# Retention and attention scores in 128-row products throughout, and the Fourier products ahead of the key projection

## The chip, the core and the metric

The kernel runs on one core of a Trainium2 chip. The metric is the device time of one execution in microseconds (us). Of the kernel before there are three timed runs, 2704.53 to 2708.25 us with a median of 2707.93 us, and one profiled execution of 2709.11 us, in which the span from the first to the last instruction is 2707.0 us.

## What is computed

The reference is a backbone of two layers over 512 latent tokens and 256 context tokens of width 1024, all in float32. Each layer is a half-step SwiGLU, a token mixing of four groups of heads side by side, and a second half-step SwiGLU. The change lies in the token mixing, which in short is:

```python
pl = split(n_lat @ w_in); pc = split(n_ctx @ w_in)      # ten groups of columns
# retention, 4 heads of 64: rotary q, k; decay both ways around each token
scores = einsum('bhcld,bhcmd->bhclm', qc, kc) * intra
o      = einsum('bhclm,bhcme->bhcle', scores, vc) + carried state
fft_lat = real(fft2(pl[4]))                             # over tokens and over 64 features
# attention: 4 query heads, 2 key heads, RMS norm and rotary on q and k
s = einsum('bkgqd,bknd->bkgqn', q, k) * HEAD_DIM ** -0.5
o = einsum('bkgqn,bknd->bkgqd', softmax(s), v)          # keys: context and latent tokens
gm_lat  = gelu(u) * (w_s @ layer_norm(gelu(v)) + b_s)
mix_lat = concatenate([ret_lat, fft_lat, att_lat, gm_lat]) @ w_out
```

The context stream goes through the same mixing in layer 0; in layer 1 only the latent stream does.

## The kernel before

Nearly all matrix products work on pairs of a rounded high part and a low part (the rest), both in a 32-bit format (`fp32r`) that TensorE takes at full rate; a product of two such pairs is three products (high by high, high by low, low by high). In the trace the products of the projections, the SwiGLUs and the scores are on the lines L241 and L243 (of the helper `mm`), transposes on L282, and all that VectorE (DVE), ScalarE (ACT) and GpSimd (POOL) do on L127.

The scores use a packing of their own. A head has 64 features, so half of the 128 rows of a product would be empty. `stack` (line 1485) takes the transposed heads, two in one PSUM bank of 128 partitions, and fills tiles for them. For keys the 64 rows of a head's own half hold the high part and the other 64 rows the low part (`lo is None`: two copies on ACT, two subtractions on DVE). For queries all 128 rows of `keys` hold the high part twice (four copies), and the low part goes into the 64 rows of the head's own half of `lo` (two subtractions). A score tile is then two products into one bank: one over 128 rows (high and low parts of the keys by the high part of the queries) and one over 64 rows, the slice `b0:b0 + 64` (high part of the keys by the low part of the queries). In retention the keys are the stationary operand and 512 latent (or 256 context) queries stream; in attention 128 queries are stationary and up to 512 keys stream, so that a tile of 768 keys is a product of 512 and one of 256 columns, each with its 64-row partner.

Per layer, `mixing` (line 1952) issues the projections in this order: retention's queries, keys and values for two pairs of heads (`qk0`, `rv`, `qk1`), the gate, the gMLP inputs, the Fourier input `f`, attention's queries `aq`, keys and values `akv`; then the Fourier products over tokens (`dft` weights), then the first half of the output projection (`wout`, sections 3 and 0) and the second (sections 1 and 2). After a projection an epilogue (rotary or norm on DVE and ACT, transposes on PE, `stack`) prepares its tiles. `ret_core`, `att_core`, `gm_core` and `four_tail` are separate tasks.

The order on each engine is decided when the program is built. A scheduler runs these tasks as generators; each waits until the times that a cost model gives for its operands are reached, and then emits its instructions. Tasks with a lower number go first, and the main sequence of projections, with the number 9, fills the time that the others leave to PE. The model counts the columns of a product and not its rows. Long-lived tiles come out of 20 slots of one size (`uget`, `uf`); a task that finds none free waits. Weights are read in the order of `wplan` (line 486), at most four blocks ahead.

Of the kernel before, what the change touches and what calls it, by code (L numbers as in the profile page):

```python
# [15 lines left out]
P = 128  # L16
# [19 lines left out]
def f32v(ap):  # L36
    return ap.bitcast(F32)
# [103 lines left out]
class Kernel:  # L141
# [344 lines left out]
    def wplan(self):  # L486
# [86 lines left out]
        for l in range(2):  # L573
            ffn(l, 1)
            win(l, "qk0", [(0, 128), (256, 128)])
            win(l, "rv", [(512, 256)])
            win(l, "qk1", [(128, 128), (384, 128)])
            win(l, "rg", [(768, 256)])
            win(l, "gu", [(1792, 256)])
            win(l, "gv", [(2048, 256)])  # L580
            win(l, "f", [(1024, 256)])
            win(l, "aq", [(1280, 256)])
            win(l, "akv", [(1536, 256)])
            dft(l)
            wout(l, (3, 0))
            wout(l, (1, 2))
            ffn(l, 2)
# [897 lines left out]
    def stack(self, keys, lo, src):  # L1485

        own = (slice(0, 64), slice(64, 128))
        yield self.at(src)  # L1490
        for h in range(2):
            self.A("copy", keys[own[h], h], src[own[h]])
        if lo is not None:
            for h in range(2):
                self.A("copy", keys[own[1 - h], h], src[own[h]])
        yield self.at(keys)
        for h in range(2):
            self.V("tensor_sub", keys[own[1 - h], h] if lo is None else lo[own[h]], src[own[h]], f32v(keys[own[h], h]))

    def turn_task(self, jobs, dsts, flag):  # L1500

# [9 lines left out]
    def ret_qk(self, p):  # L1511

        def epi(t, bank, ps):
            yield (lambda: ("mc", self.layer) in self.flags)
            y, a, b = yield from self.tw(3)
            yield self.at(bank)
            yield self.vidle(self.SE)
            yv = y.rearrange("p (t c) -> p t c", t=2)
            self.rope(lambda tt: yv[:, tt].rearrange("p (h s c) -> p h s c", h=4, s=2), ps.rearrange("p t (h s c) -> p t h s c", h=4, s=2),
                      self.rrope[:, t:t + 2, 0, :], self.rrope[:, t:t + 2, 1, :], 4, a, b)  # L1520
            self.dead(bank, a, b)
            self.spawn(task(t, y, yv), 1)

        def task(t, y, yv):
            tt = slice(t * P, (t + 2) * P)
            jobs, dsts = [[yv[:, i, 128:256] for i in range(2)]], [(self.rk[p][:, :, tt], None)]
            if t < 4:
                jobs.append([yv[:, i, 0:128] for i in range(2)])
                dsts.append((self.rq[p][:, 0:2, tt], self.rq[p][:, 2, tt]))
            elif self.layer == 0:  # L1530
                jobs.append([yv[:, i, 0:128] for i in range(2)])
                dsts.append((self.rqx[:, p, 0:2], self.rqx[:, p, 2]))
            yield from self.turn_task(jobs, dsts, ("rqk", p))
            self.dead(y)
        return epi
# [25 lines left out]
    def ret_core(self, l, p):  # L1561

        if p == 1:
            yield (lambda: ("rD", l) in self.flags)
        Dn = []
        for i in range(2):
            x = yield from self.uget([P, 1536])
            yield (lambda: min(self.xdone.values()) == KT)
            yield from self.decay(l, 2 * p + i, x)
            Dn.append(x)  # L1570
        if p == 0:
            self.ro = yield from self.uget([P, 2, TOK])
            self.flags.add(("rD", l))
        yield (lambda: self.count.get(("rqk", p), 0) == 6 and self.count.get("rv", 0) == 6)
        q, k = self.rq[p], self.rk[p]
        yield self.rdy(q, k, self.rv[p], Dn[0])
        parts = [(0, 512, [4, 5, 0, 1, 2, 3])]
        if l == 0:
            parts.append((512, 256, [4, 5]))

        def soft(ps, nq, D, w0, t, ok):
            sh, sl = t
            yield self.at(ps[:, :nq])
            self.V("scalar_tensor_tensor", ps[:, :nq], ps[:, :nq], 0.125, D[:, w0:w0 + nq], op0=ALU.mult, op1=ALU.mult)
            yield from self.split_t(sh[:, :nq], sl[:, :nq], ps[:, :nq])
            self.dead(ps)
            ok.append(True)

        for i in range(2):
            h = 2 * p + i  # L1590
            b0 = 64 * i
            D = Dn[i]
            yield self.rdy(D)
            for q0, nq, keys in parts:
                po = None
                pend = []
                for ki in range(len(keys) + 2):
                    if ki < len(keys):
                        kt = keys[ki]
                        t = yield from self.tw(2, [F32R, F32R])  # L1600
                        ps = yield from self.bank()
                        kk = slice(kt * P, (kt + 1) * P)
                        qx = q if q0 == 0 else self.rqx[:, p]
                        self.mm(ps[:, :nq], k[:, i, kk], qx[:, i], True, False)
                        self.mm(ps[:, :nq], k[b0:b0 + 64, i, kk], qx[b0:b0 + 64, 2], False, True)
                        w0 = 896 + 128 - (kt - 4) * P if kt >= 4 and q0 == 0 else 384 - (kt % 4) * P
                        ok = []
                        self.spawn(soft(ps, nq, D, w0, t, ok), 1)
                        pend.append((ki, kt, t, ok))
                        yield  # L1610
                    if len(pend) > self.RP or ki >= len(keys) and pend:
                        kj, kt, t, ok = pend.pop(0)
                        if po is None:
                            po = yield from self.bank()
                        yield (lambda: ok)
                        yield self.rdy(t[1][:, :nq])
                        self.mmv(po[:, :nq], self.rv[p][:, kt, i], t[0][:, :nq], t[1][:, :nq], kj == 0, kj == len(keys) - 1)
                        self.dead(t[0], t[1])
                        yield
                self.spawn(self.ret_fold(l, p, self.ro[b0:b0 + 64, p, q0:q0 + nq], po[:, :nq]), 1)  # L1620
            self.uf(Dn[i])
        self.uf(self.rq[p], self.rk[p], self.rv[p])
        if p == 1 and l == 0:
            self.uf(self.rqx)

    def ret_fold(self, l, p, dst, po):
        yield from self.fold(dst, po)
# [52 lines left out]
    def att_qk(self, l, which):  # L1680
# [13 lines left out]
        def task(t, x, sq):  # L1694
# [34 lines left out]
            if which == 0:  # L1729

                jobs = [[y[:, i, j * P:(j + 1) * P] for i in range(2)] for j in range(2)]
                dsts = [(self.aq[j][:, :, tt], self.aq[2][:, j, tt]) for j in range(2)]
            else:
                jobs = [[y[:, i, 0:128] for i in range(2)]]
                dsts = [(self.ak[:, :, tt], None)]
# [5 lines left out]
    def att_core(self, l):  # L1741
# [10 lines left out]
        def scores():  # L1752
            for it, (t0, nk, h) in enumerate(its):
                yield (lambda: it - done["t"] < 4)
                b0 = 64 * (h // 2)
                kv = h // 2
                k0 = 0 if nk == 768 else 512
                for tt in range(2):
# [5 lines left out]
                    for c0 in range(0, nk, 512):  # L1764
                        c1 = min(c0 + 512, nk)
                        ks = slice(k0 + c0, k0 + c1)
                        self.mm(ps[:, c0:c1], self.aq[h % 2][:, kv, qs], self.ak[:, kv, ks], True, False)
                        self.mm(ps[:, c0:c1], self.aq[2][b0:b0 + 64, h % 2, qs], self.ak[b0:b0 + 64, kv, ks], False, True)
                    self.spawn(soft(it, tt, pa[it % 4][:, tt, :nk], ps, nk), 1)
                    yield  # L1770

# [180 lines left out]
    def mixing(self, l, norm):  # L1952
# [20 lines left out]
            self.count["rv"] = self.count.get("rv", 0) + 2  # L1973

        for p in range(2):
            self.rq[p] = yield from self.uget([P, 3, 512], F32R)
            self.rk[p] = yield from self.uget([P, 2, TOK], F32R)
            if p == 0 and l == 0:
                self.rqx = yield from self.uget([P, 2, 3, 256], F32R)
            if p == 0:  # L1980
                self.spawn(self.ret_core(l, 0), 2)
                for i in range(2):
# [86 lines left out]
            self.count["f"] = self.count.get("f", 0) + 2  # L2069

        yield from self.proj(l, [("f", epi_f, t) for t in lat])
        self.aq = yield from self.ugets(3, [P, 2, TOK], F32R)
        qk = self.att_qk(l, 0)
        yield from self.proj(l, [("aq", qk, t) for t in lat])
        self.ak = yield from self.uget([P, 2, TOK], F32R)
        self.av = yield from self.uget([P, 6, 2, 2, 64], F32R)
        kv = self.att_qk(l, 1)
        yield from self.proj(l, [("akv", kv, t) for t in every])
        for k in range(4):
            self.uf(*self.xt[k])  # L2080
        self.spawn(self.att_core(l), 2)
        chunks = [LAT, CTXC] if l == 0 else [LAT]
# [18 lines left out]
        if l == 0:  # L2101
# [9 lines left out]
            self.A("copy", self.fT[:, :, 512:768], ps.rearrange("p (e c) -> p e c", e=2))  # L2111
            self.dead(ps)
        self.uf(fh, fl)
        self.spawn(self.four_tail(l), 2)
        yield (lambda: ("mix", l, 3) in self.flags and ("mix", l, 0) in self.flags)
        yield from self.wout(l, (3, 0), chunks, G)
# [135 lines left out]
```

## Time and profile before

| | |
|---|---|
| median of three timed runs | 2707.93 us |
| profiled execution | 2709.11 us |
| its span | 2707.0 us |
| PE busy (matmuls) | 2611.7 us, 96% |
| weight loads (PEld) | 2442.5 us, 90% |
| DVE / ACT / POOL busy | 74% / 47% / 50% |
| token mixing, layer 0 and layer 1 | about 608 to 954 us and 2050 to 2326 us |

A matmul's end is modelled in the profile, so that a busy PE may still be waiting between two products. Whether it does is read from the distance between the starts of neighbouring rows of the timeline, and from the idle time ahead of a weight load on PEld: every product has one load of its own.

### The profile page before, as it was taken

To read this page: it belongs to the slowest core of one execution; us is meant where nothing else is said; L and a number is where in the kernel's file an instruction comes from. 1 tells how busy PE (TensorE), PEld (TensorE's weight loads), DVE (VectorE), ACT (ScalarE), POOL (GpSimd) and SP (SyncE) were. 2 spreads that over 40 slices of the span, in tenths; PEclk is the share of its full clock that TensorE was granted. 3 is DMA by queue.
4 is the path that set the end of the run, shared out by engine and by line. 5 is a ranking of instruction groups with operands and counts; after the bars stand their busy time and mean duration, and the time that the engine had idled before them with its cause. 6 is when DMAs were issued, how large, how long until landed. Compare 5 with 4: busy or idle time off the path is not lost.

```text
span 2707.0 us, 45375 instructions
## 1 busy us (share of the span) xinstructions
PE 2611.7 (96%) x17308; PEld 2442.5 (90%) x17308; DVE 2014.0 (74%) x3473; ACT 1269.3 (47%) x2620; POOL 1345.2 (50%) x1094
## 2 busy tenths in 40 slices
PE   7999999999999999999999989999999999999998
PEld 5888999998797988888999989999999797999998
DVE  5765787877578785656887877878878677877776
ACT  5433444455645554343444534444446545544445
POOL 3535666733222253546765547668734231654443
PEclk9999999999999999999999999999999999999999
DMA  8456222121111145553123111221232111122332
GB/s 289 138 167 210 71 70 87 63 81 55 51 44 47 40 144 191 172 187 109 63 63 102 55 47 63 64 93 63 63 104 63 51 60 42 48 94 94 105 99 78
DMA packets 242778, 252.62 MB, mean 93 GB/s; under 512 B 12188, under 2 KB 226432, under 8 KB 242560
## 3 DMA queue, kind: packets, MB, share of 16 engines
q1 hardware_dynamic: 236304, 246.82, 28.5%
q10 hardware_dynamic: 6256, 2.90, 0.4%
q8 instruction: 136, 2.23, 0.3%
q14 instruction: 82, 0.67, 0.1%
HBM read 247.59 MB, written 2.10 MB: 92 GB/s over the span
## 4 chain that ended last, share of the span: by engine, by line
PE 72%; DVE 18%; issue 3%; ACT 2%; DMA 2%; POOL 2%; SPq 0%; ACTq 0%; DVEq 0%; POOLq 0%
PE b L241 41%; PE b L243 28%; DVE u L127 7%; DVE w L127 6%; DVE t L127 3%; PE b L254 2%; PE b L282 2%; DVE H L127 2%; DMA raw<-in_ffn_w_gu_dram 1%; ACT w L127 1%; DMA u<-in_ada_w_dram 1%; ACT u L127 1%; ACT t L127 1%; POOL u L127 0%; POOL raw L127 0%
## 5 line engine op out<-in xcount | busy, mean ns | idle before, releaser
L241 PE MATMUL b<-u,w 128*128 128x384 f32 (+1 forms) x8736 | 1465.3, 326 | 30.7 <-DVE u L127 21.4
L241 PEld LDWEIGHTS b<-u,w 128*128 128x128 f32 x8736 | 1424.0, 189 | 61.0 <-DVE u L127 28.9
L127 ACT CAST w<-raw 128x512 fp32r<-128x512 f32 x949 | 578.9, 621 | 626.9 <-PE b L241 255.2
L127 DVE TENSOR_TENSOR w<-raw,w 128x512 fp32r<-128x512 f32 x688 | 663.0, 972 | 231.4 <-ACT w L127 219.6
L127 POOL TENSOR_TENSOR raw<-raw 128x512 f32<-128x512 f32 x416 | 616.9, 1504 | 397.2 <-DMA raw<-in_ffn_w_gu_dram 138.1
L127 POOL TENSOR_TENSOR w<-raw,w 128x512 fp32r<-128x512 f32 x261 | 371.0, 1433 | 543.6 <-ACT w L127 495.2
L243 PE MATMUL b<-u,w 128*128 128x256 f32 (+2 forms) x3888 | 590.9, 309 | 17.7 <-ACT u L127 5.8
L243 PEld LDWEIGHTS b<-u,w 128*128 128x128 f32 x3888 | 543.0, 194 | 44.8 <-issue 10.2
L127 DVE SCALAR_TENSOR_TENSOR H<-b,modG,H 128x128 f32<-128x128 f32 (+3 forms) x832 | 368.5, 474 | 154.1 <-PE b L243 85.4
L243 PE MATMUL b<-w,u 128*128 128x256 f32 x2172 | 286.6, 288 | 1.8 <-DVE w L127 1.8
L243 PEld LDWEIGHTS b<-w,u 128*128 128x128 f32 x2172 | 270.0, 192 | 12.0 <-issue 6.8
L127 ACT COPY t<-b 128x384 f32<-128x384 f32 (+5 forms) x287 | 123.5, 431 | 209.6 <-PE b L241 98.1
L127 ACT CAST u<-u 128x384 fp32r<-128x384 f32 (+4 forms) x318 | 140.8, 464 | 121.1 <-DVE u L127 103.1
L127 DVE TENSOR_TENSOR u<-u 128x384 fp32r<-128x384 f32 (+8 forms) x227 | 183.0, 819 | 12.9 <-ACT u L127 12.1
L127 POOL TENSOR_TENSOR u<-u 128x384 fp32r<-128x384 f32 (+2 forms) x137 | 123.0, 907 | 93.2 <-ACT u L127 92.5
L243 PE MATMUL b<-u 128*64 128x256 f32 (+7 forms) x516 | 141.1, 371 | 0.0
L127 DVE TENSOR_TENSOR t<-t,b 128x384 f32<-128x384 f32 (+3 forms) x216 | 106.2, 494 | 43.3 <-PE b L241 42.3
L127 POOL TENSOR_TENSOR nacc<-nacc,t 128x256 f32<-128x256 f32 (+2 forms) x112 | 89.7, 802 | 95.6 <-ACT t L127 91.6
L127 ACT CAST u<-t 128x384 fp32r<-128x384 f32 (+2 forms) x162 | 74.1, 471 | 114.1 <-DVE t L127 107.3
L243 PEld LDWEIGHTS b<-u 128*128 128x128 f32 (+2 forms) x516 | 81.6, 176 | 47.0 <-issue 34.4
L127 ACT CAST u<-b 64x256 fp32r<-64x256 f32 (+3 forms) x175 | 77.9, 454 | 75.3 <-PE b L282 72.7
L127 POOL TENSOR_TENSOR rs<-mse,mhalf 128x2 f32<-128x2 f32 (+4 forms) x41 | 45.1, 1104 | 115.4 <-DVE mse L127 106.1
(95 smaller groups left out, 1660.7 us busy)
## 6 DMA issues: line engine op xcount, KB each, us to landing
raw<-in_ffn_w_gu_dram SPq DMA_DIRECT2D x176, 512.0 KB
adaraw<-in_ada_w_dram SPq DMA_DIRECT2D x113, 512.0 KB
raw<-in_ffn_w_down_dram SPq DMA_DIRECT2D x88, 512.0 KB
raw<-in_w_in_dram SPq DMA_DIRECT2D x28, 512.0 KB
raw<-in_w_out_dram SPq DMA_DIRECT2D x32, 256.0 KB
u<-in_ada_w_dram SPq DMA_DIRECT2D x15, 512.0 KB
u<-in_ada_w_dram SPq DMA_DIRECT2D x16, 384.0 KB
raw<-in_w_in_dram SPq DMA_DIRECT2D x16, 256.0 KB
```

The source lines that it names most:

```text
L127: getattr(self.eng, name)(*args, **kw)
L241: self.nc.tensor.matmul(out, a, b, start=start, stop=stop, skip_group_check=True)
L243: self.nc.tensor.matmul(out, a, b, start=start, stop=stop)
L254: self.nc.tensor.matmul(out[q:q + 32], self.cs[:, k], x, start=start, stop=stop)
L282: self.nc.tensor.transpose(out, in_, self.ident[:p, :p])
```

## The change

The low part of the queries is stored twice, in both halves of its tile, so that the second product of a score tile also runs over 128 rows; it then also adds low part of the keys by low part of the queries. `stack` makes four subtractions instead of two for queries. Retention's queries take two tiles of `[128, 2, 768]` per pair of heads in the place of one of `[128, 3, 512]` and, in layer 0, one for both pairs' context queries (`rqx`); attention's queries take four tiles in the place of three. The Fourier products with their weights come ahead of the projection `akv`, and the tiles for attention's keys and values are taken after them.

```diff
@@ wplan
             win(l, "aq", [(1280, 256)])
+            dft(l)
             win(l, "akv", [(1536, 256)])
-            dft(l)
@@ stack
-        for h in range(2):
-            self.V("tensor_sub", keys[own[1 - h], h] if lo is None else lo[own[h]], src[own[h]], f32v(keys[own[h], h]))
+        if lo is None:
+            for h in range(2):
+                self.V("tensor_sub", keys[own[1 - h], h], src[own[h]], f32v(keys[own[h], h]))
+        else:
+            for h in range(2):
+                for o in range(2):
+                    self.V("tensor_sub", lo[own[o], h], src[own[h]], f32v(keys[own[h], h]))
@@ ret_core
-                        qx = q if q0 == 0 else self.rqx[:, p]
-                        self.mm(ps[:, :nq], k[:, i, kk], qx[:, i], True, False)
-                        self.mm(ps[:, :nq], k[b0:b0 + 64, i, kk], qx[b0:b0 + 64, 2], False, True)
+                        self.mm(ps[:, :nq], k[:, i, kk], q[0][:, i, q0:q0 + nq], True, False)
+                        self.mm(ps[:, :nq], k[:, i, kk], q[1][:, i, q0:q0 + nq], False, True)
@@ att_core, scores
                         self.mm(ps[:, c0:c1], self.aq[h % 2][:, kv, qs], self.ak[:, kv, ks], True, False)
-                        self.mm(ps[:, c0:c1], self.aq[2][b0:b0 + 64, h % 2, qs], self.ak[b0:b0 + 64, kv, ks], False, True)
+                        self.mm(ps[:, c0:c1], self.aq[2 + h % 2][:, kv, qs], self.ak[:, kv, ks], False, True)
@@ mixing
-            self.rq[p] = yield from self.uget([P, 3, 512], F32R)
+            self.rq[p] = yield from self.ugets(2, [P, 2, TOK], F32R)
             self.rk[p] = yield from self.uget([P, 2, TOK], F32R)
-            if p == 0 and l == 0:
-                self.rqx = yield from self.uget([P, 2, 3, 256], F32R)
...
-        self.aq = yield from self.ugets(3, [P, 2, TOK], F32R)
+        self.aq = yield from self.ugets(4, [P, 2, TOK], F32R)
         qk = self.att_qk(l, 0)
         yield from self.proj(l, [("aq", qk, t) for t in lat])
-        self.ak = yield from self.uget([P, 2, TOK], F32R)
-        self.av = yield from self.uget([P, 6, 2, 2, 64], F32R)
-        kv = self.att_qk(l, 1)
-        yield from self.proj(l, [("akv", kv, t) for t in every])
...
-        self.spawn(self.att_core(l), 2)
...
         self.fT = yield from self.uget([P, 2, TOK])
...
         self.uf(fh, fl)
+        self.ak = yield from self.uget([P, 2, TOK], F32R)
+        self.av = yield from self.uget([P, 6, 2, 2, 64], F32R)
+        kv = self.att_qk(l, 1)
+        yield from self.proj(l, [("akv", kv, t) for t in every])
...
+        self.spawn(self.att_core(l), 2)
...
         self.spawn(self.four_tail(l), 2)
```

On DVE, ahead of the first retention score of layer 0, `u<-b,u 64x256` are the subtractions of `stack`, `t<-b,u` and `t<-t` rotary, `w<-raw,w` the low parts of weights, and the last row belongs to the first score tiles. Before:

```order
L127 TENSOR_TENSOR u<-b,u 64x256 x2
L127 TENSOR_TENSOR w<-raw,w 128x512 x2
L127 TENSOR_TENSOR t<-b,u 128x8x32 x4
L127 TENSOR_TENSOR t<-t 128x4x32 x4
L127 TENSOR_TENSOR w<-raw,w 128x512
L127 TENSOR_TENSOR u<-b,u 64x256 x2
L127 TENSOR_TENSOR w<-raw,w 128x512
L127 TENSOR_TENSOR u<-b,u 64x256 x2
L127 TENSOR_TENSOR w<-raw,w 128x512
L127 TENSOR_TENSOR u<-b,u 128x4x64 x2
L127 SCALAR_TENSOR_TENSOR b<-b,u 128x512 x2
```

and with the change:

```order
L127 TENSOR_TENSOR u<-b,u 64x256 x4
L127 TENSOR_TENSOR w<-raw,w 128x512 x2
L127 TENSOR_TENSOR t<-b,u 128x8x32 x4
L127 TENSOR_TENSOR t<-t 128x4x32 x4
L127 TENSOR_TENSOR w<-raw,w 128x512
L127 TENSOR_TENSOR u<-b,u 64x256 x2
L127 TENSOR_TENSOR w<-raw,w 128x512
L127 TENSOR_TENSOR u<-b,u 64x256 x4
L127 TENSOR_TENSOR u<-b,u 128x4x64 x2
L127 TENSOR_TENSOR w<-raw,w 128x512
L127 SCALAR_TENSOR_TENSOR b<-b,u 128x512 x2
```

The subtractions behind the queries' transposes go from two to four in place; the others stay as they are, and one subtraction for weights moves behind the values'.

On PE, from the end of the key projection of layer 0 to the first attention scores (`b<-u 128x512 x2`), `b<-w,u 128x256` are the projection and, last, the Fourier products, `b<-ident,t` the transposes of the epilogues, 128x257 to 128x127 the Fourier transform's second stage (`four_tail`), and `b<-u,w` the output projection. Before:

```order
L243 MATMUL b<-w,u 128x256 x48
L282 MATMUL b<-ident,t 128x128 x2
L243 MATMUL b<-w,u 128x256 x12
L243 MATMUL b<-u 128x257
L243 MATMUL b<-u 128x255
L243 MATMUL b<-u,w 128x512 x6
L282 MATMUL b<-ident,t 128x128 x2
L243 MATMUL b<-u 128x129
L243 MATMUL b<-u 128x127
L243 MATMUL b<-u 128x257
L243 MATMUL b<-u 128x255
L243 MATMUL b<-u 128x129
```

and with the change:

```order
L243 MATMUL b<-w,u 128x256 x36
L243 MATMUL b<-u 128x257
L243 MATMUL b<-u 128x255
L243 MATMUL b<-u 128x129
L243 MATMUL b<-u 128x127
L282 MATMUL b<-ident,t 128x128 x2
L243 MATMUL b<-u 128x257
L243 MATMUL b<-u 128x255
L243 MATMUL b<-u 128x129
L243 MATMUL b<-u 128x127
L243 MATMUL b<-u,w 128x512 x12
L243 MATMUL b<-u,w 128x256 x6
```

Before, the run of 48 ends in 24 Fourier products, and the run of 12 behind the next transposes is the rest of the 36. In the change the 36 at the top are the last key products alone: the Fourier products have gone, and `four_tail` and the output projection come up to the transposes.

SP issues the reads of weights; `in_k_dft` are the Fourier weights. Before:

```order
L391 DMA raw<-in_w_in_dram 128x4x128 x4
L391 DMA raw<-in_w_in_dram 128x4x256 x12
L391 DMA raw<-in_k_dft_dram 128x2x256 x3
L391 DMA raw<-in_w_out_dram 128x2x256 x16
L391 DMA raw<-in_ffn_w_gu_dram 128x4x256 x4
```

and with the change:

```order
L391 DMA raw<-in_w_in_dram 128x4x128 x4
L391 DMA raw<-in_w_in_dram 128x4x256 x10
L391 DMA raw<-in_k_dft_dram 128x2x256 x3
L391 DMA raw<-in_w_in_dram 128x4x256 x2
L391 DMA raw<-in_w_out_dram 128x2x256 x16
L391 DMA raw<-in_ffn_w_gu_dram 128x4x256 x4
```

The Fourier weights go ahead of the last two blocks of the input projection (`akv`); the rest keeps its order.

## Rows read from the trace of the kernel before

**Rows 1.** Page, section 1: busy time, share and instructions of each engine.

```profile
PE 2611.7 (96%) x17308; PEld 2442.5 (90%) x17308; DVE 2014.0 (74%) x3473; ACT 1269.3 (47%) x2620; POOL 1345.2 (50%) x1094
```

**Rows 2.** Groups by form on PE, whole span: shapes, count, busy, mean; idle before.

```profile
L243 PE MATMUL b<-u 64*128 64x512 f32 x80 | 39.6, 495 | 0.0
...
L243 PE MATMUL b<-u 64*128 64x256 f32 x48 | 18.3, 382 | 0.0
```

**Rows 3.** Timeline of PE, retention, layer 0: start, length, what, count.

```profile
711.27 0.82 PE L243 MATMUL b<-u 128*128 128x512 f32 x2
712.02 0.97 PE L243 MATMUL b<-w,u 128*128 128x256 f32 x6
712.83 0.62 PE L243 MATMUL b<-t,u 128*64 128x512 f32 x2
713.28 0.82 PE L243 MATMUL b<-u 128*128 128x512 f32 x2
```

**Rows 4.** Timeline of weight loads (PEld), same stretch; idle before in brackets.

```profile
711.60 0.18 PEld L243 LDWEIGHTS b<-u 64*128 64x128 f32 x1 [0.36 <-issue]
712.02 0.77 PEld L243 LDWEIGHTS b<-w,u 128*128 128x128 f32 x6 [0.24 <-issue]
```

**Rows 5.** Timeline of PE, retention over context, layer 0.

```profile
696.18 1.22 PE L243 MATMUL b<-u 128*128 128x256 f32 x4
697.33 2.42 PE L243 MATMUL b<-u,w 128*128 128x256 f32 x18
699.59 0.63 PE L243 MATMUL b<-t,u 128*128 128x256 f32 x4
```

**Rows 6.** Timeline of PE, attention, layer 0.

```profile
849.42 1.45 PE L243 MATMUL b<-u 128*128 128x512 f32 x4
850.80 0.98 PE L243 MATMUL b<-u,w 128*128 128x256 f32 x6
```

**Rows 7.** Windows: stretch, length; busy (instructions) per engine; PEclk; DMA share, GB/s.

```profile
640.00:750.00 110.00, 108.07 (x657) 87.26 (x657) 70.47 (x143) 62.35 (x119) 24.23 (x27) 1.00 0.17 51
797.00:835.80 38.80, 35.80 (x270) 33.48 (x267) 34.47 (x82) 26.21 (x62) 14.90 (x11) 1.00 0.25 83
835.80:917.90 82.10, 82.10 (x467) 63.85 (x466) 64.78 (x124) 44.34 (x96) 10.11 (x8) 1.00 0.06 20
2084.00:2172.00 88.00, 86.07 (x494) 67.99 (x493) 57.78 (x110) 46.41 (x86) 19.65 (x23) 0.98 0.19 60
2237.00:2302.00 65.00, 65.00 (x342) 48.88 (x341) 49.45 (x81) 34.56 (x66) 10.29 (x9) 0.97 0.12 38
```

**Rows 8.** Groups by form on DVE, 835.8 to 917.9 (attention, layer 0).

```profile
L127 DVE TENSOR_TENSOR u<-b,u 128x768 fp32r<-128x768 f32 x16 | 15.2, 952 | 3.9 <-ACT u L127 3.8
...
L127 DVE TENSOR_TENSOR t<-b,t 64x256 f32<-64x256 f32 x10 | 4.1, 413 | 1.8 <-ACT t L127 1.7
...
L127 DVE RECIPROCAL sm<-sm 128x1 f32<-128x1 f32 x24 | 3.7, 155 | 1.7 <-ACT u L127 1.7
```

**Rows 9.** The same, 2237 to 2302 (attention, layer 1).

```profile
L127 DVE TENSOR_TENSOR u<-b,u 128x768 fp32r<-128x768 f32 x15 | 14.1, 954 | 7.7 <-ACT u L127 7.6
```

**Rows 10.** The same, 600 to 850: subtractions of the stacks.

```profile
L127 DVE TENSOR_TENSOR u<-b,u 64x256 fp32r<-64x256 f32 x42 | 17.7, 422 | 11.8 <-ACT u L127 11.1
```

**Rows 11.** Timeline of DVE ahead of the first retention score, layer 0.

```profile
633.79 1.63 DVE L127 TENSOR_TENSOR u<-b,u 64x256 fp32r<-64x256 f32 x4 [2.23 <-ACT u L127]
...
638.17 1.41 DVE L127 TENSOR_TENSOR w<-raw,w 128x512 fp32r<-128x512 f32 x2 [1.13 <-ACT w L127]
...
648.75 0.86 DVE L127 TENSOR_TENSOR u<-b,u 64x256 fp32r<-64x256 f32 x2 [1.24 <-ACT u L127]
```

**Rows 12.** Timeline of PE around the last key-projection epilogues, layer 0.

```profile
824.10 0.51 PE L282 MATMUL b<-ident,t 128*128 128x128 f32 x2 [1.58 <-DVE t L127]
...
829.47 0.53 PE L282 MATMUL b<-ident,t 128*128 128x128 f32 x2 [1.17 <-DVE t L127]
```

**Rows 13.** Groups on ACT, whole span: function-table loads.

```profile
L127 ACT ACT_TABLE_LOAD x16 | 20.5, 1283 | 1.5 <-DVE cs L665 1.2
```

More of the change, by code (lines that the diff above doesn't have):

```diff
@@ L1526, in task @@
             jobs, dsts = [[yv[:, i, 128:256] for i in range(2)]], [(self.rk[p][:, :, tt], None)]
-            if t < 4:
+            if t < 4 or self.layer == 0:
                 jobs.append([yv[:, i, 0:128] for i in range(2)])
[L1529 to L1532, printed above, removed]
+                dsts.append((self.rq[p][0][:, :, tt], self.rq[p][1][:, :, tt]))
             yield from self.turn_task(jobs, dsts, ("rqk", p))
@@ L1575, in ret_core @@
         q, k = self.rq[p], self.rk[p]
-        yield self.rdy(q, k, self.rv[p], Dn[0])
+        yield self.rdy(*q, k, self.rv[p], Dn[0])
         parts = [(0, 512, [4, 5, 0, 1, 2, 3])]
@@ L1621, in ret_core @@
             self.uf(Dn[i])
-        self.uf(self.rq[p], self.rk[p], self.rv[p])
-        if p == 1 and l == 0:
-            self.uf(self.rqx)
+        self.uf(*self.rq[p], self.rk[p], self.rv[p])
     def ret_fold(self, l, p, dst, po):
@@ L1731, in task @@
                 jobs = [[y[:, i, j * P:(j + 1) * P] for i in range(2)] for j in range(2)]
-                dsts = [(self.aq[j][:, :, tt], self.aq[2][:, j, tt]) for j in range(2)]
+                dsts = [(self.aq[j][:, :, tt], self.aq[2 + j][:, :, tt]) for j in range(2)]
             else:
@@ L1754, in scores @@
                 yield (lambda: it - done["t"] < 4)
-                b0 = 64 * (h // 2)
                 kv = h // 2
@@ L2071, in mixing @@
         yield from self.proj(l, [("f", epi_f, t) for t in lat])
-        self.aq = yield from self.ugets(3, [P, 2, TOK], F32R)
+        self.aq = yield from self.ugets(4, [P, 2, TOK], F32R)
         qk = self.att_qk(l, 0)
         yield from self.proj(l, [("aq", qk, t) for t in lat])
-        self.ak = yield from self.uget([P, 2, TOK], F32R)
-        self.av = yield from self.uget([P, 6, 2, 2, 64], F32R)
-        kv = self.att_qk(l, 1)
-        yield from self.proj(l, [("akv", kv, t) for t in every])
-        for k in range(4):
-            self.uf(*self.xt[k])
-        self.spawn(self.att_core(l), 2)
-        chunks = [LAT, CTXC] if l == 0 else [LAT]
         self.fT = yield from self.uget([P, 2, TOK])
@@ L2113, in mixing @@
         self.uf(fh, fl)
+        self.ak = yield from self.uget([P, 2, TOK], F32R)
+        self.av = yield from self.uget([P, 6, 2, 2, 64], F32R)
+        kv = self.att_qk(l, 1)
+        yield from self.proj(l, [("akv", kv, t) for t in every])
+        for k in range(4):
+            self.uf(*self.xt[k])
+        self.spawn(self.att_core(l), 2)
+        chunks = [LAT, CTXC] if l == 0 else [LAT]
         self.spawn(self.four_tail(l), 2)
```

## The prediction

> **What bounds the kernel now.** I read the busy times first, then the products by form, then PE's timeline in the token mixing beside that of its weight loads, and last the windows and DVE's groups in the stages that the change touches. PE shows 2611.7 us of the 2707.0 us span [rows 1], so most of what PE is spared comes off the end, unless another engine takes its place. But the matmul rows end where a model puts their end, so a busy PE can hide waiting. The reader is to see it in the score pairs. A pair of 512 columns begins at 711.27 and the next row at 712.02, which is 0.75 us; two products of the same 512 columns that also add into one bank, but use all rows, begin at 712.83 and are followed at 713.28, which is 0.45 us [rows 3]. The weight loads show why: the load for the 64-row product begins 0.36 us after the load before it has ended, and the load behind it waits 0.24 us more, while six loads for 128-row products follow each other without a pause [rows 4]. So PE empties itself before and after each 64-row product. There are 80 of them with 512 columns and 48 with 256 [rows 2], and the order holds the same 128 score products in the change, all over 128 rows.
>
> **What the change takes off PE.** A pair of 512 columns: 0.75 less 0.45, 0.30 us [rows 3]. For 256 columns a product of a long run costs 2.26 us by 18, 0.126 us (697.33 to 699.59); two score pairs take 697.33 less 696.18, 1.15 us, in the place of four times 0.126, so a pair gives back 0.32 us [rows 5]. In attention a tile of 768 keys is a group of four, 1.38 us (849.42 to 850.80) [rows 6] in the place of 0.45 and twice 0.126, 0.70 us; it gives back 0.68 us. The counts come from the loops. Retention has 4 heads by 6 key blocks, 24 pairs of 512 a layer, and in layer 0 another 4 by 2, 8 pairs of 256: 24 x 0.30 + 8 x 0.32 = 9.8 us in layer 0 and 7.2 us in layer 1. Attention has 2 query groups by 4 heads by 2 tiles, 16 groups of four a layer, and in layer 0 another 8 pairs of 256: 16 x 0.68 + 8 x 0.32 = 13.5 us and 10.9 us. In all that is 41.4 us of PE's time.
>
> **What of it reaches the end.** In retention DVE is busy 70.5 of 110.0 us and ACT 62.4 (layer 0), DVE 57.8 of 88.0 us in layer 1 [rows 7]. With 9.8 us less of PE's time and 5.1 us more for DVE (below), DVE has 75.6 of 100 us. PE remains the bound there, and I take the 17.0 us whole; the projections of the gate and the gMLP stand between the scores and fill PE.
>
> In attention it does not stay so. Layer 0 takes 82.1 us, in which DVE is busy 64.8 us [rows 7] and stands idle another 7.2 us for results of ACT (3.8 + 1.7 + 1.7) [rows 8], which a faster PE doesn't shorten. PE would need 82.1 - 13.5 = 68.6 us, DVE 64.8 + 7.2 = 72.0 us. So DVE is late next, and the stage gives 82.1 - 72.0 = 10.1 us. In layer 1 PE needs 65.0 - 10.9 = 54.1 us, DVE 49.5 us [rows 7] and 7.6 us of waits for ACT [rows 9], 57.1 us: it gives 7.9 us. The bounds are nothing (DVE's other waits stay as well) and 13.5 and 10.9 us (ACT's results come earlier too). I take 18.0 us for both.
>
> **What it adds.** `stack` subtracts twice more for each pair of query tiles: 12 of them in layer 0 (6 of retention, 6 of attention), 8 in layer 1, so 40 more subtractions of 64x256 at 0.422 us [rows 10], 16.9 us on DVE. Where they stand decides what they cost.
>
> Ahead of the first retention score the doubled ones stand behind the transposes of the queries. DVE is idle there for 2.23 and 1.13 us, waiting for ACT [rows 11], and that takes up those of the first two query blocks. The last block's stand right in front of the score (the row at 648.75, which becomes four): 2 x 0.42 = 0.84 us, and behind them wait the values' subtractions and the first score tiles on DVE. Between nothing (the projection goes on on PE) and 0.84 us a layer I take the latter, 1.7 us. The second pair of heads has its stacks beside whole projections and costs nothing.
>
> Attention's stand where DVE has least to spare, 34.5 us busy of 38.8 between the query epilogues and the first score [rows 7], and there the Fourier products have moved. In layer 0 PE waits for DVE 1.58 us and 1.17 us at the transposes of the last two key blocks [rows 12]. By the order 24 Fourier products, 24 x 0.126 = 3.0 us, precede the first of these, so it comes due about 4.6 us after the last key product; with the change four short products of `four_tail` stand there (at least 0.5 us), and PE would wait 4.1 us. At the second, 5.4 us later, there are four more of them, 12 products of 512 (12 x 0.225 by rows 3) and 6 of 256, 4.0 us, a wait of 1.4 us. Together 5.5 us in the place of 2.75. Against that, 36 Fourier products (4.5 us) now run ahead of the key products, in which DVE can work off the 12 added subtractions (5.1 us). So the term lies between -2.75 us (the waits go) and 9.6 us (4.5 + 5.1, nothing hidden); the row that it is nearest to is the wait of today, and I take 2.4 us. For layer 1, with 8 subtractions (3.4 us) and 24 Fourier products (3.0 us), between -2.4 and 6.4, I take 2.1 us. What comes due late is the first attention score; the output projection's products are pulled ahead of it and fill PE meanwhile.
>
> The order also has 19 function-table loads on ACT in the place of 16, since the second pair's decay tables now fall among the gMLP's activations: 3 x 1.28 us [rows 13], hidden under PE's projections, as ACT is busy 62 of 110 us there [rows 7]; if that cover is gone, 3.9 us. The Fourier weights are read before the last key weights instead of after, the same reads two places earlier on SP; DMA is busy 25% there or less [rows 7], so I count nothing. More slots are held by queries (two more tiles at most in retention, one in attention), and a task might wait for one; the order shows the second retention core starting behind more of the gMLP projection, with PE's work in between, so I count nothing; the other end is one more wait like those of today's transposes, 1.6 us [rows 12].
>
> **The sum.** 17.0 + 18.0 - 1.7 - 4.5 = 28.8 us off the profiled execution of 2709.1 us gives 2680.3 us. The median of the timed runs lies 1.2 us below that execution, so the prediction is 2679 us, 1.1% faster.
>
> **The rivals.**
>
> All of it comes through: ACT's results come earlier with PE's, DVE holds attention up nowhere, and the key epilogues cost no more than now. Then 41.4 less 1.7 and some 3 us goes off, 2707.9 - 36.7 = 2671 us. For it speaks that most of DVE's idle time in attention is not put down to ACT; against it that DVE would have to be busy 94% of the stage (64.8 of 68.6).
>
> Attention gives nothing: DVE in its fixed order takes over at once with all its present waits, and the two stages stay at 82.1 and 65.0 us. Then 17.0 - 1.7 - 4.5 = 10.8 us remain, 2697 us. For it speaks that the order is set by a model that counted these score products without the gaps, so that DVE's work is already planned as tightly as it may be; against it that PE is without a gap for those whole stages (82.1 of 82.1 busy) and DVE idle for 17 of them.
>
> The gap stays: it belongs to any second product whose rows of the array are those of the one before, not to the change between 64 and 128 rows. Then the score pairs are as long as before, the change doesn't do on PE what its diff says, and only the added work counts: 1.7 + 4.5 us, 2714 us, slower. It decides from the first score pair on, at every one of the 128. Against it speak the six loads without a pause, and the pairs of 0.45 us, all on products over 128 rows [rows 3, 4]. The Trainium skill has a rule by which it would come out so: "TensorE: Matmul & The Clock Gate" (Part 3, Packing small matmuls, what overlaps and what doesn't) says that a weight load overlaps a running product only where the two use different row groups. By that rule two 128-row products would never overlap and the change would gain nothing; the trace of this kernel shows otherwise, 0.126 us a product with loads in unbroken sequence, and I give it little.
>
> **How the numbers follow.** The forecast has 0.56, with 2672 to 2692 as its own range (attention between 10 and 23 us, the key stage between 0 and 10). All comes through 0.16, attention gives nothing 0.18, the gap stays 0.04; 0.06 is for a mishap of the new order that I don't see, half of it within 0.2% and half slower. The range for 8 in 10, 2667 to 2698 us, takes in the two rivals on the fast side and leaves out what would be slower. Faster by over 0.2% (5.4 us, about what a measurement of this kernel tells from no change) is then 0.56 + 0.16 + 0.17 = 0.89; within 0.2% gets 0.01 from attention's rival and 0.03 from the mishap, 0.04; slower 0.07.
>
> **What would show it.** Score pairs of 512 columns about 0.45 us apart, groups of four about 0.70 us, and no pause of the weight load in them; pairs still at 0.75 us make the whole forecast wrong. Attention of layer 0 near 72 us from its first score to the last product, with DVE about 90% busy and waits of PE for DVE or ACT where there are none now; at 69 us the first rival holds, at 80 us the second. The waits at the last two key transposes near 5 us in layer 0, and 116 subtractions of 64x256 in the place of 76. If PE's clock, 1.00 in most of these windows and 0.97 and 0.98 in layer 1 [rows 7], falls in longer waits, that is a cost that I have not counted; halved for 4 us it would take about 2 us.

## The result, and the profile after

The changed kernel takes 2676.53 us, the median of four runs (2671.01 to 2678.99), against 2706.23 us for the kernel before on the same chip: a ratio of 0.9888, interval [0.9869, 0.9907], 29.7 us or 1.1% faster. The forecast was 2679 us. Its profiled execution was the shortest of the four, 2671.01 us, so that the profiles lie 38.1 us apart; some 8 us of what the stages below show is the chance of these two executions. A run of the same kernel as a control gave 2674.74 us, ratio 0.9883 [0.9868, 0.9898].

The busy times of the page, to be set against [rows 1]:

```profile
PE 2565.5 (96%) x17308; PEld 2438.3 (91%) x17308; DVE 2031.5 (76%) x3508; ACT 1273.7 (48%) x2623; POOL 1349.7 (51%) x1099
```

PE has lost 46.2 us with the same number of products. Its groups by form over the whole span show why: the groups of 64 rows of [rows 2] are gone, and their 128 products are in these two, of 128 rows.

```profile
L243 PE MATMUL b<-u 128*128 128x512 f32 x168 | 54.5, 415 | 2.2 <-DVE u L127 2.2
...
L243 PE MATMUL b<-u 128*128 128x256 f32 x212 | 48.6, 294 | 0.6 <-DVE u L127 0.3 <-ACT u L127 0.2
```

PE's timeline, at the pair of [rows 3], at the two context pairs of [rows 5] and at a group of four of [rows 6] (start, length, what, count):

```profile
688.64 0.64 PE L243 MATMUL b<-u 128*128 128x256 f32 x4
689.11 2.32 PE L243 MATMUL b<-u,w 128*128 128x256 f32 x18
...
711.26 0.62 PE L243 MATMUL b<-u 128*128 128x512 f32 x2
711.72 0.63 PE L243 MATMUL b<-t,u 128*64 128x512 f32 x2
...
835.07 0.86 PE L243 MATMUL b<-u 128*128 128x512 f32 x4
835.76 1.54 PE L243 MATMUL b<-u,w 128*128 128x512 f32 x6
```

The pair takes 0.46 us in the place of 0.75, two context pairs 0.47 in the place of 1.15, the group 0.69 in the place of 1.38. The weight loads of that group, to be set against [rows 4], where a retention pair has pauses of 0.36 and 0.24 us around its 64-row load:

```profile
834.95 0.78 PEld L243 LDWEIGHTS b<-u 128*128 128x128 f32 x4
835.65 1.22 PEld L243 LDWEIGHTS b<-u,w 128*128 128x128 f32 x6
```

No row of it has idle time before it. The time by stage follows from the starts of rows on PE: the first projection product of the mixing, the first score of retention, its last value product (from here to attention is the key stage below), the first score of attention, and the transposes of the next norm. All figures are in us; "forecast" is the sum of the prediction's terms for the same stretch. The last column is needed because the stages do not hold the same products: in the order of the change 6 products of the output projection in layer 0 and 12 in layer 1 stand ahead of attention and no longer in it. At 0.225 us each they are 1.4 and 2.7 us, and the column gives the gain with them counted where they were.

| | before | after | gained | forecast | gained, same products |
|---|---|---|---|---|---|
| layer 0, up to attention | 43.8 + 91.4 + 92.8 | 43.8 + 89.5 + 85.0 | 9.7 | 6.6 | 11.1 |
| layer 0, attention | 96.1 | 82.2 | 13.9 | 10.1 | 12.5 |
| layer 1, up to attention | 43.6 + 75.5 + 68.1 | 42.2 + 75.2 + 69.2 | 0.6 | 4.3 | 3.3 |
| layer 1, attention | 77.1 | 66.0 | 11.1 | 7.9 | 8.4 |

The groups of these products in the attention stage of layer 1, before and after (one more of each reaches in from the stage ahead):

```profile
L243 PE MATMUL b<-u,w 128*128 128x512 f32 x73 | 20.9, 429 | 0.0
...
L243 PE MATMUL b<-u,w 128*128 128x512 f32 x61 | 15.6, 394 | 0.0
```

The 43.6 us of layer 1 before were at a granted clock of 0.96, the 42.2 after at 1.00; the order of before, with attention's products sorted (below), takes 42.2 us there at 1.00, so that some 1.5 us of that gain are the clock of one execution.

Attention gave most of what PE was spared, 12.5 of 13.5 us in layer 0 and 8.4 of 10.9 in layer 1. The windows from its first score to its last product, to be set against the third and fifth of [rows 7] (PE, PEld, DVE, ACT, POOL busy, PEclk):

```profile
824.99:893.50 68.51, 66.91 (x461) 60.48 (x460) 62.17 (x125) 42.65 (x94) 9.26 (x8) 1.00 0.11 32
...
2210.90:2265.00 54.10, 50.93 (x332) 45.68 (x331) 48.55 (x82) 34.00 (x65) 9.00 (x8) 0.97 0.15 46
```

Layer 0 takes 68.5 us, 69.9 with the six products (forecast 72.0, first rival 69). DVE is busy 91% of it, as foreseen, but stops PE for only 0.8 us. In layer 1 it is 54.1 us, 56.8 with the twelve products, close to the forecast of 57.1; PE, which had no wait there before, waits 2.5 us for DVE and 0.6 for ACT. DVE's groups in the window of layer 0 answer to [rows 8]; the last column but one is the idle time before them:

```profile
L127 DVE TENSOR_TENSOR u<-b,u 128x768 fp32r<-128x768 f32 x16 | 15.1, 950 | 1.0 <-ACT u L127 1.0
...
L127 DVE TENSOR_TENSOR t<-b,t 64x256 f32<-64x256 f32 x10 | 4.1, 413 | 1.7 <-ACT t L127 1.6
...
L127 DVE RECIPROCAL sm<-sm 128x1 f32<-128x1 f32 x24 | 3.7, 154 | 0.5 <-ACT u L127 0.4
```

DVE's waits for ACT in these three groups fell from 7.2 to 3.0 us. ACT itself had waited for PE's transposes (L282), which stand behind the scores in PE's queue. Its costliest copies in the same windows, before:

```profile
L127 ACT CAST u<-b 128x768 fp32r<-128x768 f32 x16 | 12.7, 802 | 14.8 <-PE b L282 14.8
```

and after:

```profile
L127 ACT CAST u<-b 128x768 fp32r<-128x768 f32 x16 | 12.7, 801 | 8.1 <-PE b L282 7.9
```

The idle time ahead of them is nearly halved, and their results reach DVE earlier.

The key stage of layer 0 still has PE's waits at the transposes [rows 12], smaller and spread:

```profile
793.18 0.64 PE L282 MATMUL b<-ident,t 128*128 128x128 f32 x2 [1.45 <-DVE t L127]
...
815.52 0.51 PE L282 MATMUL b<-ident,t 128*128 128x128 f32 x2 [0.97 <-DVE t L127]
...
821.38 0.33 PE L282 MATMUL b<-ident,t 128*128 128x128 f32 x1 [0.46 <-DVE t L127]
```

With 0.15 and 0.42 us more at 808 they are 3.5 us, where the forecast had 5.5 and before 2.9. Layer 1 gained 11.7 us in all where 12.2 were forecast. At the end of its retention, in its key stage and in attention new waits stand:

```profile
2138.66 0.68 PE L243 MATMUL b<-t,u 128*64 128x512 f32 x2 [0.45 <-DVE t L127]
2139.85 0.68 PE L243 MATMUL b<-t,u 128*64 128x512 f32 x2 [0.52 <-DVE t L127]
2141.73 1.11 PE L243 MATMUL b<-t,u 128*64 128x512 f32 x2 [1.20 <-DVE t L127]
...
2201.83 0.51 PE L282 MATMUL b<-ident,t 128*128 128x128 f32 x2 [1.97 <-ACT t L127]
...
2251.46 1.65 PE L243 MATMUL b<-u 128*128 128x512 f32 x4 [1.91 <-DVE u L127]
```

In the whole mixing of layer 1 PE's listed waits are 11.8 us, before 5.2 us.

The subtractions of 64x256 are 66 up to the first attention score of layer 0 in the place of 42 [rows 10], at the same 422 ns, in DVE's groups by form from 600 to 830:

```profile
L127 DVE TENSOR_TENSOR u<-b,u 64x256 fp32r<-64x256 f32 x66 | 27.8, 422 | 9.1 <-ACT u L127 8.1
```

ACT's groups have 19 table loads in the place of 16 [rows 13].

### The profile page after: what moved, and what is told of

It reads as the page before. It is cut to its first block, busy times and chain, and to the rows that moved or that the text cites. A ratio compares the mean times of both kernels' runs of the same rounds, so it can differ in the third digit from the quotient of the medians.

```text
span 2669.1 us, 45429 instructions
## 1 busy us (share of the span) xinstructions
PE 2565.5 (96%) x17308; PEld 2438.3 (91%) x17308; DVE 2031.5 (76%) x3508; ACT 1273.7 (48%) x2623; POOL 1349.7 (51%) x1099
## 3 DMA queue, kind: packets, MB, share of 16 engines
q1 hardware_dynamic: 236304, 246.82, 29.7%
## 4 chain that ended last, share of the span: by engine, by line
PE 69%; DVE 21%; issue 3%; ACT 3%; POOL 2%; DMA 2%; SPq 0%; DVEq 0%; ACTq 0%; POOLq 0%
PE b L241 40%; PE b L243 24%; DVE u L127 8%; DVE w L127 6%; DVE t L127 4%; PE b L254 2%; DVE H L127 2%; PE b L282 2%; ACT w L127 1%; DMA raw<-in_ffn_w_gu_dram 1%; ACT u L127 1%; POOL raw L127 1%; POOL u L127 1%; ACT t L127 1%; DMA u<-in_ada_w_dram 1%
## 5 line engine op out<-in xcount | busy, mean ns | idle before, releaser
L127 DVE TENSOR_TENSOR w<-raw,w 128x512 fp32r<-128x512 f32 x688 | 671.1, 985 | 239.0 <-ACT w L127 226.9
L243 PE MATMUL b<-w,u 128*128 128x256 f32 x2172 | 279.2, 285 | 1.9 <-DVE w L127 1.8
L127 POOL TENSOR_TENSOR u<-u 128x384 fp32r<-128x384 f32 (+3 forms) x139 | 124.9, 908 | 96.5 <-ACT u L127 95.9
L127 POOL TENSOR_TENSOR nacc<-nacc,t 128x256 f32<-128x256 f32 (+2 forms) x112 | 89.7, 801 | 103.5 <-ACT t L127 99.5
L243 PE MATMUL b<-u 128*128 128x256 f32 (+5 forms) x516 | 104.4, 336 | 3.4 <-DVE u L127 3.1
L127 DVE TENSOR_TENSOR u<-b,u 64x256 fp32r<-64x256 f32 (+3 forms) x175 | 91.0, 525 | 20.1 <-ACT u L127 18.3
```

The source lines that it names most:

```text
L127: getattr(self.eng, name)(*args, **kw)
L243: self.nc.tensor.matmul(out, a, b, start=start, stop=stop)
```

## The experiments

My theory was the prediction's: the pause belongs to the change between products of 128 and of 64 rows; the rows are the whole gain and all else costs. The rivals: the pause belongs to any 64-row product; the order makes the gain; the subtractions, or the Fourier move, make the cost. Ratios are to the kernel before, with their intervals; the four of one set (the first four below) had 2707.91 us for it, the others 2706.2 to 2706.7.

**The rows taken back**, all, in attention, in retention, and the Fourier move alone on the kernel before:

```diff
-  self.mm(ps[:, :nq], k[:, i, kk], q[1][:, i, q0:q0 + nq], False, True)
+  self.mm(ps[:, :nq], k[b0:b0 + 64, i, kk], q[1][b0:b0 + 64, i, q0:q0 + nq], False, True)
-  self.mm(ps[:, c0:c1], self.aq[2 + h % 2][:, kv, qs], self.ak[:, kv, ks], False, True)
+  self.mm(ps[:, c0:c1], self.aq[2 + h % 2][64 * kv:64 * kv + 64, kv, qs], self.ak[64 * kv:64 * kv + 64, kv, ks], False, True)
```

> The changed kernel with the second score products back on 64 rows: 116 subtractions, the new tiles and the new order stay. Theory: all of the gain goes, and the added work shows alone, by the prediction's terms 1.7 + 4.5 us: 2712 us, pairs at 0.75 us, groups of four at 1.38 us. Rival (order, or the double storage itself, brings the gain): 2675 to 2690 us.

> The changed kernel with only attention's second score products back on 64 rows. Theory by the prediction's terms: 24.4 us of PE's gaps come back against the changed kernel if attention gave its whole 24.4 us there, 18 us if DVE held it: 2694 to 2701 us. Rival (what is spared in attention is lost elsewhere): within 10 us of the changed kernel.

> The changed kernel with only retention's second score products back on 64 rows. Theory: 17.0 us of gaps come back, 2693 us. Rival (retention's gain is partly lost in layer 1, whose trace shows new waits of PE for DVE at the end of retention, 0.45, 0.52 and 1.20 us): 10 us or less, 2683 to 2687 us.

> The kernel before with one part of the change alone: the Fourier products and their weights ahead of the key projection; products, tiles and subtractions as before. Theory (the gain is PE's gaps at the 64-row products): those gaps stay, so the time is the one of before within 4 us, 2704 to 2710 us, and score pairs of 512 columns stay 0.75 us long. Rival (the new order made the gain): 2680 us or so.

Measured: all on 64 rows 2722.17 us, 1.0053 [1.0036, 1.0069]; retention alone on 128 rows 2702.47, 0.9981 [0.9970, 0.9992]; attention alone 2694.73, 0.9952 [0.9938, 0.9967]; the move alone 2713.23, 1.0023 [1.0014, 1.0032]. From the 64-row version retention's rows give 19.7 us and attention's 27.4, and both together some 45 (2722.2 less 2676.5, from two sets). The move by itself gives nothing. On 64 rows all else in the change costs 14.3 us, 5.3 of them the move; both lie above what was expected (2712, and 2704 to 2710 us).

Where these 14.3 us are is seen in the windows of the mixing. First the 64-row version, both attention stages, then the kernel before:

```profile
836.94:935.03 98.09, 96.67 (x576) 77.77 (x574) 71.45 (x144) 48.31 (x107) 13.95 (x14) 0.98 0.14 44
...
2249.36:2329.38 80.02, 77.66 (x432) 61.09 (x430) 55.43 (x95) 38.18 (x75) 12.76 (x13) 0.94 0.10 32
```

```profile
835.80:931.90 96.10, 96.06 (x581) 77.60 (x580) 73.18 (x142) 49.42 (x109) 15.49 (x15) 1.00 0.12 39
...
2237.14:2314.24 77.10, 77.10 (x444) 61.02 (x443) 55.51 (x94) 38.41 (x76) 14.61 (x15) 0.98 0.10 32
```

Each stage is 2 to 3 us longer, although 1.4 and 2.7 us of products have gone ahead of it, PE waits 1.4 and 2.4 us in it, and the granted clock is lower. With these products the two attention stages cost some 9 us more than before. Over the eight stages of both mixings PE is busy 584.8 us in the place of 576.9 and idle 19.4 in the place of 11.5: half of the cost is waits, half longer products, most of it at the lower clock. Over the timed runs of that set the mean granted clock is 0.988 in the 64-row version and in the move alone, and 0.9905 before. By my estimate these 0.0025 of 2707 us are up to 6.8 us, as much as the whole cost of the move; whether the clock fell by chance or because of the new waits isn't shown.

**Is it the change of rows?** In the kernel before, attention's four products in another order, 128, 128, 64, 64 rows:

```diff
+  for lo in range(2):
       for c0 in range(0, nk, 512):
+          # lo 0: the product over 128 rows; lo 1: the one over 64 rows
```

> The kernel before, with attention's products of a score tile in another order: the two over 128 rows (512 and 256 columns), then the two over 64 rows. Theory of the switch (PE empties itself when the rows of the array change): two changes a group in the place of four, so a group goes from 1.38 to about 1.04 us, 32 groups give 32 x 0.34 = 10.9 us of PE's time and the time is near 2697 us. Theory of the 64-row product (each pays its own 0.3 us whatever its neighbour, or two loads of the same rows never overlap): the group stays at 1.38 us and the time at 2707.

2695.86 us, 0.9956 [0.9941, 0.9971]: 10.4 us less with the same products. PE's timeline at one group, and that of the weight loads at the next:

```profile
845.79 1.05 PE L243 MATMUL b<-u 128*128 128x512 f32 x4
846.77 0.98 PE L243 MATMUL b<-u,w 128*128 128x256 f32 x6
```

```profile
847.47 0.31 PEld L243 LDWEIGHTS b<-u 128*128 128x128 f32 x2
848.03 0.29 PEld L243 LDWEIGHTS b<-u 64*128 64x128 f32 x2 [0.25 <-issue]
848.57 3.31 PEld L243 LDWEIGHTS b<-u,w 128*128 128x128 f32 x18 [0.25 <-issue]
```

The group takes 0.98 us. Two 64-row loads stand behind each other without a pause, and so do two of 128 rows; the pause is at the change alone, once each way. The theory of the switch holds, that of the 64-row product falls.

**Are the subtractions the cost?** The low part stored once, the other half of its tile set to zero by GpSimd when it is taken; then the order of the change on 64 rows without the added subtractions; then the zeros again, with the planner still counting the subtractions, so that PE's order is the change's, product for product:

```diff
-  for o in range(2):
-      self.V("tensor_sub", lo[own[o], h], src[own[h]], f32v(keys[own[h], h]))
+  self.V("tensor_sub", lo[own[h], h], src[own[h]], f32v(keys[own[h], h]))
+  # and, for the zeros, on each low tile when it is taken, for both h:
+  self.G("tensor_scalar", t[64 - 64 * h:128 - 64 * h, h], <mhalf, broadcast>, 0.0, None, op0=ALU.mult)
```

> The changed kernel with the low part of the queries stored once; the other half of its tile is set to zero by GpSimd when the tile is taken, so that the 128-row product adds nothing there. DVE has 76 subtractions of 64x256 again. Theory of the subtractions (the 40 added ones are what the change pays beside the Fourier move, about 8 us by the 64-row version of it): 2668 us. Theory of tiles and order (the wider tiles and the order that follows from them are what is paid): 2676 us, as the changed kernel, or up to 2 us more for GpSimd's writes.

> The changed kernel with second products over 64 rows and the low part stored once: the order and tiles of the change without its rows and without its added subtractions. Its 64-row version with the subtractions took 2722.2 us, the Fourier move alone 2713.2. Theory of the subtractions: 2714 us, the Fourier move's time. Theory of tiles and order: 2722 us.

> The changed kernel with the added subtractions left out and the other half of the low tiles set to zero by GpSimd, as in the earlier run with zeros, but with the planner still counting the subtractions: PE has the order of the change, product for product, and DVE the same order less 40 subtractions of 0.42 us, 16.9 us. Theory that the subtractions cost what the 64-row versions show (3 us), or their waits in layer 1 do: 2673 us, with shorter waits of PE for DVE at the last key transposes. Theory that they are hidden everywhere: 2676 us. A rival: GpSimd's writes slow DVE's work down at the same time, 2678 us or more.

Zeros 2675.57 us, 0.9884 [0.9864, 0.9904], no change; 64 rows with the low part once 2719.11, 1.0042 [1.0028, 1.0056], not to be told from 1.0053; zeros in the change's order 2688.71, 0.9934 [0.9920, 0.9948], 14 us slower than the control of its set, with 16.9 us less on DVE. The rival of the last one holds, and in two ways. DVE is busy 2021.3 us in the place of 2031.5, 10.2 less and not 16.9, so that its other work took longer. Set against the control's mean of the same forms, about half of that time stands in instructions that ran beside a write; why the rest took longer stays open. And the writes stand in GpSimd's own queue. Its timeline at the start of the mixing of layer 1, and PE's wait there:

```profile
2028.45 4.85 POOL L1513 TENSOR_SCALAR u<-mhalf 64x768 fp32r<-64x768 f32 x2
2033.28 0.71 POOL L127 TENSOR_TENSOR nacc<-nacc,t 128x256 f32<-128x256 f32 x1
```

```profile
2036.21 0.69 PE L282 MATMUL b<-ident,nacc 128*128 128x128 f32 x2 [4.15 <-POOL nacc L127]
```

The norm's sums stand behind the zeros and PE behind the sums: up to the first retention score layer 1 takes 49.4 us in the place of 42.2 to 43.6, and layer 0 47.3 in the place of 43.8. The key stage of layer 1 takes 72.9 in the place of 69.2. What the subtractions cost is seen in layer 0 behind that point, where 18 of them (7.6 us on DVE) are gone: retention, key stage and attention take 89.7, 84.4 and 82.2 us, with them 89.5, 85.0 and 82.2. There they are hidden; what the 6 ahead of that point and the 16 of layer 1 cost, this run can't tell.

**Layer 1.** The Fourier products behind the key projection in layer 1 alone, with attention's queries in three tiles to make room for it (the 128 rows wholly without the move have no run); and, for the waits at the end of its retention, the change with shorter statistics ahead of them on DVE:

```diff
-  self.V("bn_stats", st, xv[:, i, :])
+  self.V("bn_stats", st, xv[:, i, :32], cost=self.V.fixed + 256 / self.V.rate)
```

> The changed kernel with the Fourier products of layer 1 behind the key projection again (and read there); attention's queries of layer 1 lie in three tiles of 3x512 in the place of four, which makes the room. Layer 0 is as in the change. Theory that the Fourier move costs layer 1 its key stage (72.5 against 68.1 us in the move alone): 4 us less, 2672 us. Theory that the subtractions or the new order in retention of layer 1 make the waits: 2676 us or a little more, since four fewer products cover the query stacks.

> The changed kernel in exactly its order, with the gMLP's statistics taken over 32 of 256 columns (the rest of that sum is left out), so that each of 10 takes some 0.15 us on DVE in the place of 0.41. In layer 1 two of them stand ahead of the last three value products of retention, where PE waited 0.45, 0.52 and 1.20 us and its clock fell to 0.50 behind the waits. Theory that DVE's queue makes these waits and the waits the clock: the 1.20 us wait falls to 0.7 or less, the clock stays at 1.00 behind it, 2 to 3 us less, 2674 us. Theory that the products' own chain (ACT's rounding, then DVE) makes them: the waits stay and so does the time, 2676 us.

> The changed kernel once more, as a control beside the other two on the same chip: 2676 us, between 2671 and 2680; its ratio to the kernel before 0.989.

2673.25 us, 0.9879 [0.9861, 0.9897]; 2676.37, 0.9884 [0.9869, 0.9898]; the control 2674.74. All three are one time. The move late gives layer 1 nothing (69.2 us for its key stage, as in the change). PE's timeline with the short statistics, and behind it the control's:

```profile
2137.28 0.68 PE L243 MATMUL b<-t,u 128*64 128x512 f32 x2 [0.52 <-DVE t L127]
2138.69 0.68 PE L243 MATMUL b<-t,u 128*64 128x512 f32 x2 [0.73 <-DVE t L127]
...
2141.63 2.27 PE L243 MATMUL b<-u 128*128 128x256 f32 x6 [0.69 <-DVE u L127]
```

```profile
2140.95 0.68 PE L243 MATMUL b<-t,u 128*64 128x512 f32 x2 [0.51 <-DVE t L127]
2142.83 0.68 PE L243 MATMUL b<-t,u 128*64 128x512 f32 x2 [1.19 <-DVE t L127]
...
2145.77 2.27 PE L243 MATMUL b<-u 128*128 128x256 f32 x6 [0.69 <-DVE u L127]
```

DVE's queue makes the third wait (1.19 to 0.73 us), not the first two; and a wait of 0.69 us follows all the same. Half a microsecond taken from one wait doesn't show in the time. Nor do such waits lower the clock by themselves: the control has the same three and stays at 1.00 behind them.

**A version of the best parts**: layer 0 with the zeros, layer 1 with the late Fourier products.

> The best of the parts seen, together: layer 0 with the low part stored once and zeros from GpSimd (counted by the planner, as in the first run with zeros), layer 1 with the subtractions, three tiles for attention's queries and the Fourier products behind the key projection. By the profiles of the two, layer 0's mixing takes 298.9 us in the place of 300.5 and layer 1's 253.4 in the place of 252.6 to 254.2: 2673 us, ratio to before 0.988, not to be told from the changed kernel's 0.9883 to 0.9888. If the orders add up as they do in the single runs it may reach 2671; if a new order makes new waits, 2680.

2673.13 us, 0.9876 [0.9859, 0.9892]. This version can't be told from the changed kernel either.

## Why the prediction was right, and where it was not

**PE's gain: mechanism right, size low.** The single pair and the group came as forecast, to 0.01 us, and the two context pairs to 0.03; the loads have no pause. But the terms were taken from a pair by itself. Where pairs follow each other a pair costs more. PE's timeline at the first three of retention and at two groups of attention, before:

```profile
651.61 2.54 PE L243 MATMUL b<-u 128*128 128x512 f32 x6
654.08 1.70 PE L243 MATMUL b<-w,u 128*128 128x256 f32 x12
...
843.05 2.91 PE L243 MATMUL b<-u 128*128 128x512 f32 x8
845.89 1.66 PE L243 MATMUL b<-u,w 128*128 128x512 f32 x6
```

and after:

```profile
650.53 1.55 PE L243 MATMUL b<-u 128*128 128x512 f32 x6
651.92 1.59 PE L243 MATMUL b<-w,u 128*128 128x256 f32 x12
...
830.21 1.56 PE L243 MATMUL b<-u 128*128 128x512 f32 x8
831.60 0.82 PE L282 MATMUL b<-ident,u 128*128 128x128 f32 x6
```

Three pairs went from 2.47 to 1.39 us, 0.36 a pair, two groups from 2.84 to 1.39, 0.73 a group. If all stood so, the sum would be 48 x 0.36 + 16 x 0.32 + 32 x 0.73 = 45.8 us in the place of 41.4; the runs gave some 45.

**Attention: a step that failed in layer 0.** "DVE is late next" gave 18.0 us. The rows taken back gave 27.4, but against a version whose attention stages cost some 9 us more than those of before. Against the kernel before the stages gave 12.5 and 8.4 us, where 10.1 and 7.9 were forecast. In layer 0 I took DVE's waits for ACT as fixed, and they shrank from 7.2 to 3.0 us, so that DVE held PE up for 0.8 us and not for 3.4; the first rival had this right. In layer 1 the term came out, and PE waits there for DVE as it says, 2.5 us. Retention was taken whole, 17.0 us, and gave 19.7.

**What it adds: too low.** 6.2 us were forecast, 14.3 measured on 64 rows. By these runs there are two errors of opposite sign, some 10 us (35 forecast for the rows, 45 measured) and 8 us, and it is luck that they left 2679 beside 2676.5. The costs aren't where I had put them: up to the first retention score no stage got longer (43.8 us both times, 43.6 and 42.2), and layer 0's key stage has 0.6 us of waits more, not the 2.75 worked out there (of which the sum took 2.4 without a reason). Layer 1 has 6.6 us more of waits, along with a lower clock in its key stage (0.95, before 1.00), in a new order of the whole stage, which I had counted at nothing. Which part of the change makes that order's cost stays open: the Fourier move alone costs 5.3 us on 64 rows, yet with 128 rows neither its undoing in layer 1 nor the missing subtractions (with GpSimd's zeros in their place) gave anything back. The part of the prediction that failed there is "I count nothing" for the slots and the second retention core.

**The rivals.** "Attention gives nothing" fell by 68.5 us (69.9 with the same products) against 82.1. "The gap stays" fell twice: in the change, and where 64-row products stand together. The Trainium skill's rule for it ("TensorE: Matmul & The Clock Gate", Part 3, Packing small matmuls, the list of what overlaps) has loads overlap a running product only with other row groups; the text ahead of that list also allows loads into a background weight buffer. The trace does not agree with the list as it stands: here 128-row loads run beside 128-row products without a pause, 0.69 us for a group of 1536 columns.

## What to carry to other kernels

Look at the distance between the starts of products and at the idle time ahead of weight loads, not at PE's busy share: going to 64 rows and back cost 0.3 to 0.4 us a pair here. The same rows throughout, even with half of them adding nothing, give it back; sorting attention's products by their rows gave back 10.4 us. When stages are compared, count first whether they still hold the same products. Measure such a gap in runs of these products too, not only at one by itself. When PE got faster, DVE's waits for what PE feeds got shorter as well; they were no floor.

## What the runs showed that I had not expected

The low clock can stand in the place of a wait. The stretch behind the third wait in layer 1, in the changed kernel and in its control, same products:

```profile
2142.00:2144.00 2.00, 2.00 (x9) 1.81 (x9) 1.97 (x4) 0.58 (x1) 1.41 (x1) 0.50 0.00 0
...
2141.73:2147.11 5.38, 5.38 (x17) 3.67 (x18) 4.61 (x7) 1.22 (x2) 1.68 (x2) 0.68 0.29 97
```

```profile
2142.83:2147.93 5.10, 4.39 (x17) 2.30 (x17) 4.62 (x7) 1.21 (x2) 1.69 (x2) 1.00 0.34 103
```

With the clock at 0.50, the level of 1.2 GHz, for at least 2 us after the three waits (0.68 in the mean of the stretch), the changed kernel is without a wait and takes 5.38 us; at 1.00 the control waits 0.69 us and takes 5.10. And a write of zeros of 64x768 took GpSimd 2.1 to 2.7 us, so that filling half a tile with nothing took longer than DVE's subtraction of real numbers into it, three of 0.42 us.
